# Keys kept in SBUF and chunk values landed by DMA in a hybrid Conformer/RWKV-7 step

## The chip, the core and the metric

The kernel runs on one core of a Trainium2 chip. The metric is device time in microseconds (us) of one execution. The engines are TensorE (PE, with its weight loads as PEld), VectorE (DVE), ScalarE (ACT), GpSimd (POOL) and SyncE (SP). ACT, POOL and SP also issue DMAs; an issue stands in the issuing engine's order of instructions, and in the profile it is listed as ACTq, POOLq or SPq. An engine runs its instructions in order.

## The reference

One inference step of two layers with D = 1024 over 1048 tokens: 16 meta tokens, 1024 prompt tokens and 8 decode tokens. Layer 0 mixes tokens by a Conformer convolution, layer 1 by RWKV-7; each is followed by a squared-ReLU MLP with 4096 hidden features. The change lies in layer 1, whose mixer is, cut to what matters:

```python
xr, xw, xk, xv, xa, xg = (h + (prev - h) * x_mix[i] for i in range(6))
r, k, v = xr @ w_r, xk @ w_k, xv @ w_v
decay = exp(-exp(w_log(xw)));  a = sigmoid(a0 + (xa @ a1) @ a2);  g = sigmoid(xg @ g1) @ g2
kk = k * k_k;  kk = kk / max(norm_per_head(kk), 1e-12)
k = k * (1 + (a - 1) * k_a)
def _wkv7_step(S, inp):                       # per token, per head: S is 64 x 64
    sa = einsum('bhvk,bhk->bhv', S, -kk_t)
    S = S * w_t + sa[..., None] * (kk_t * a_t) + v_t[..., None] * k_t
    y = einsum('bhvk,bhk->bhv', S, r_t)
out = ((groupnorm(y) + sum(r * k * r_k) * v) * g) @ w_o
```

There are 16 heads of 64. All inputs and outputs are float32.

## The kernel before

Layer 0 takes the profile up to about 1128 us. From there to about 1840 us runs the mixer stage of layer 1, the part that the change touches; the MLP of layer 1 follows to the end, and the last chunks of the recurrence run under its first part, up to about 2080 us.

**Groups and blocks.** The mixer stage goes over four token groups (272, 256, 256 and 264 tokens) and in each over 8 blocks `p` of 128 features (`mixer_in`, the loop at L1046). A block computes the projections `pr` (r, copied by ACT at L1049) and `pv` (v, copied to `vv` at L1067), low-rank gate, decay and rate (`l_g`, `l_w`, `l_a` at L964, from `lg`, `lw`, `la`), and from them the operands of the recurrence, which go to DRAM: `d_ab` (four 64-token operands per chunk), `d_v` (values, transposed to token rows: `vt` at L1003, issue L1004; for the meta tokens `vm`, L1007 and L1008), `d_n` (the small matrices to invert), `d_g` and `d_bv`. At block 0 the low-rank projections need `p_wa`, and ACT's `lw` (L954) must be done before PE's `l_w`.

**Keys.** The keys of the next group are computed inside the current one, a block at a time (`keys`, L872): PE projects `pk`, ACT copies it to `st` (L885), issues a DMA to the DRAM tensor `d_k` (L886) and squares it to `sq` (L888); PE sums the squares per head into `pn` (L880), and the group's inverse norms `r16` come from that. In the next group `fetch` loads a block's keys from `d_k` into slot 1 of `rk2` (SP, L1042), one block ahead. DVE then makes `nkk` (L1073, from the keys and the norms), the products `kb` (one multiply of double width, L1092) and `rk` (L1095), and packs `ab` (L1104, L1105).

**Chunks.** The recurrence runs over 17 chunks: chunk 0 holds the meta tokens, the others 64 tokens each. Two operands hold a chunk's values: `sv` is state above values, `uv` is U above values; each has four quarters, a half of 64 partitions for each of two head parities, and the values fill the other half. `front(c)` loads a chunk's operands on SP: `xa`, `bk`, `p` (the inverse) and `vt`, the values as two half tiles (L1185). `chunk(c)` copies them on ACT, two copies into `sv` and two into `uv` (L1246, L1247), then runs W (L1260, reads `sv`), U (into `uv`, L1277 and L1278), S (L1285, reads `uv`), Y (L1292 reads `sv`, L1295 reads `uv`), the output `yt` (L1297) to DRAM `d_y` (two issues, L1300), and the new state into `sv` (L1303, L1306).

**Order.** On PE the mixer stage's matmuls keep the order of the program. `both()` and `fill` inside the projections call `tick`, which moves the inverses (`inverses`, on DVE), the chunks by credits (`RW`, paced by `PACE`) and the output norm on by a step. A chunk can start once its inverse has been issued (`st["inv"]`); after the end of a group the tail of its last block comes in the next group. On the other engines a scheduler orders the instructions; data loads on SP and weight loads share one queue in that order. Buffers come from pools by tag; `bufs` says how many a tag has.

```python
            for p, rk2 in ahead_of(fetch):
                both()
                ps = proj(next(wrkv), act, n, nm("r", p), both)
```

Of the kernel before, what the change touches and what calls it, by code (L numbers as in the profile page):

```python
# [16 lines left out]
P = 128  # L17
D = 1024
KT = D // P
# [29 lines left out]
def hybrid_step(tc, x_prompt, x_sample, state_conv, state_shift, state_wkv, meta_tokens,  # L49
# [10 lines left out]
    with ctx:  # L60
# [15 lines left out]
        d_hn = dram.tile([P, KT, T], F32, name="d_hn")  # L76
        d_k = dram.tile([P, KT, T], F32, name="d_k")
        d_ab = dram.tile([NCH, P, KT, 2, 2 * HS], F32, name="d_ab")
# [714 lines left out]

        prep, norm = {}, {}
        sst = cur["raw"].tile([P, D], F32, name="sst", tag="raw")
# [74 lines left out]
        def keys(g, fill):  # L870

            c0, n = G1[g]  # L872
            nm = lambda s, *a: f"{s}{g}" + "".join(f"_{x}" for x in a)
            mix = prep[g][0]
            act = [mix(2, k) for k in range(KT)]
            pn = bank(nm("pn"), "x")
            add_pn = lambda: None

            def to_pn(p, sq):
                return lambda: nc.tensor.matmul(pn[:, :n], head_sel(p), sq[:, :n], start=p == 0, stop=p == KT - 1)  # L880
            for p in range(KT):
                yield
                ps = proj(next(wrkv), act, n, nm("k", p), fill)
                k_ = pr.tile([P, N1], F32, name=nm("st", p), tag="st", bufs=2)
                nc.scalar.copy(k_[:, :n], ps[:, :n])  # L885
                nc.scalar.dma_start(d_k[:, p, c0:c0 + n], k_[:, :n])  # L886
                sq = pr.tile([P, N1], F32, name=nm("sq", p), tag="rk", bufs=2)
                nc.scalar.activation(sq[:, :n], ps[:, :n], AF.Square, scale=vec("k_k", p))  # L888
                add_pn()
                add_pn = to_pn(p, sq)  # L890
            r16 = lorap.tile([P, N1], F32, name=nm("r16"), tag="lf")
            r16p = norm[g] = [lorap.tile([P, N1], F32R, name=nm("r16" + q), tag="r16" + q, bufs=2)[:, :n] for q in "hl"]
            add_pn()
            nc.vector.tensor_scalar(r16[:, :n], pn[:, :n], L2_EPS * L2_EPS, None, op0=ALU.max)
            nc.scalar.activation(r16[:, :n], r16[:, :n], AF.Sqrt)
            nc.vector.reciprocal(r16[:, :n], r16[:, :n])
            split(*r16p, r16[:, :n], nc.vector)
        carry = {"tail": lambda: None}

        def mixer_in(g, tick):  # L900
# [13 lines left out]
            mix, hx = prep.pop(g)  # L914

            def ahead_of(load):

                nxt = load(0)
                for p in range(KT):
                    cur_, nxt = nxt, load(p + 1) if p + 1 < KT else None  # L920
                    yield p, cur_

# [64 lines left out]
            def finish(p, rk, ab, vv):  # L987
                def trace():
# [45 lines left out]
                    nc.tensor.matmul(pb[:, :n], hsum, rk[:, :n], start=True, stop=True)  # L1034
                    bv = t_("bv", p, "bv", 2)
                    nc.vector.tensor_mul(bv[:, :n], vv[:, :n], pb[:, :n])
                    return lambda: nc.gpsimd.dma_start(d_bv[:, p, c0:c0 + n], bv[:, :n])
                return trace

            def fetch(p):  # L1040
                rk2 = pr.tile([P, 3, N1], F32, name=nm("rk2", p), tag="rk2", bufs=2)
                nc.sync.dma_start(rk2[:, 1, :n], d_k[:, p, c0:c0 + n])  # L1042
                return rk2

            late, later = (lambda: lambda: None), lambda: None
            for p, rk2 in ahead_of(fetch):  # L1046
                both()
                ps = proj(next(wrkv), act, n, nm("r", p), both)
                nc.scalar.copy(rk2[:, 2, :n], ps[:, :n])  # L1049
                if p == 0:  # L1050
                    decay_rate(ww)
                if npr < n:
                    dd(p, 4, rk2[:, 2, npr:n])
                ps = lora2(wg2, p, lg, f"g{p}")
                gt = t_("gt", p, "gt", 2)
                nc.scalar.copy(gt[:, :n], ps[:, :n])
# [12 lines left out]
                later = late()  # L1069
                nkk, kp, rp = (rk2[:, i, :] for i in range(3))  # L1070
                pb = bank(nm("pb", p))
                spread(pb[:, :n], r16p, p)
                nc.vector.scalar_tensor_tensor(nkk[:, :n], kp[:, :n], nvec("k_k", p), pb[:, :n], op0=ALU.mult, op1=ALU.mult)  # L1073
                nc.vector.tensor_tensor_scan(cum[:, :n], smask[:, :n], cum[:, :n], 0.0, op0=ALU.mult, op1=ALU.add)
                em = t_("em", p, "em", 2)
                nc.scalar.activation(em[:, :n], cum[:, :n], AF.Exp, scale=DECAY_SCALE)

                ex = pr.tile([P, 5, HS + 1], F32, name=nm("ex", p), tag="ex", bufs=2)
                nc.gpsimd.memset(ex[:, :, 0:1], 1.0)
# [10 lines left out]

                kb = wa[:, :2, :n]
                nc.vector.tensor_mul(kb, rk2[:, :2, :n], kb)  # L1092
                bb, km = wa[:, 0, :], wa[:, 1, :]
                rk = t_("rk", p, "rk", 2)
                nc.vector.scalar_tensor_tensor(rk[:, :n], rp[:, :n], vec("r_k", p), km[:, :n], op0=ALU.mult, op1=ALU.mult)  # L1095

                ab = pr.tile([P, 5, 4, HS], F32, name=nm("ab", p), tag="ab", bufs=2)
                for s in segs:
                    e = ex[:, s[4]:s[4] + s[2], :s[3]]
                    e = bass.AP(e.tensor, e.offset, [*e.ap[:2], (1, 2), e.ap[2]])  # L1100
                    two = lambda t: t[:, :, s[1]:s[1] + s[2] * s[3]].rearrange("p i (c t) -> p c i t", t=s[3])
                    out = lambda i: ab[:, s[4]:s[4] + s[2], i:i + 2, :s[3]]

                    nc.vector.tensor_mul(out(0), two(rk2[:, 0:3:2, :]), e)  # L1104
                    nc.vector.tensor_mul(out(2), two(wa[:, :2, :]), cols(em, s).unsqueeze(2).broadcast_to([P, s[2], 2, s[3]]))  # L1105
# [64 lines left out]
        def front(c):  # L1170
# [10 lines left out]
            nc.sync.dma_start(p32, d_p[c].rearrange("k r t -> r k t"))  # L1181

            vt = w_([P, KT, HS], "vt", c)
            for q in range(2):
                nc.sync.dma_start(vt[HALF[1 - q]], d_v[c * HS:(c + 1) * HS, :].rearrange("t (k q v) -> q t k v", q=2, v=HS)[q])  # L1185
            yield RW[0]
# [19 lines left out]
            nc.vector.transpose(flat(x32), flat(p32))  # L1206
            chunks[c] = xa, bk, nr, no, p32, x32, vt
            yield RW[2]
# [7 lines left out]
        fronts = {}  # L1216

        def chunk(c):

            while c > st["inv"]:  # L1220
                yield None
            yield from fronts.setdefault(c, front(c))
            xa, bk, nr, no, p32, x32, vt = chunks.pop(c)
            sv, uv = st["sv"], st["uv"]

# [15 lines left out]
            for j in range(2):  # L1241
                nc.vector.tensor_scalar(p64[:, :, 32 * j:32 * j + 32], p32, par32[:, j:j + 1], None, op0=ALU.mult)

            for q in range(2):
                r = HALF[1 - q]
                nc.scalar.copy(sv[r, :, q, :], vt[r])  # L1246
                nc.scalar.copy(uv[r, :, q, :], vt[r])  # L1247

# [37 lines left out]
            if c > 0:  # L1286
# [12 lines left out]
                for q in range(2):  # L1299
                    nc.scalar.dma_start(d_y[t0:t0 + HS].rearrange("t (k q v) -> q t k v", q=2, v=HS)[q], yt[HALF[q]])  # L1300

            fs = w_([P, KT, HS], "fs", c, "w1")
            nc.vector.tensor_mul(fs, kv(ps), wend.broadcast_to([P, KT, HS]))  # L1303
# [341 lines left out]
```

## Time and profile before

| what | value |
|---|---|
| median of 3 runs | 2812.3 us (2811.88 to 2817.02) |
| the profiled execution | 2817.97 us, span 2816.3 us |
| mean granted clock of PE | 0.972 |
| DMA | 416.45 MB, 148 GB/s on average |
| 34 loads `vt` on SP, 68 copies of it on ACT | 0.562 and about 0.617 us each (median) |
| 32 issues `d_k<-st` on ACT | 0.326 us each (median) |
| 32 loads `rk<-d_k` on SP | 0.339 us each (median) |

How to read the rows: a timeline row has start and duration in us, engine, line, operation, out<-in, shape, and in brackets the idle time of that engine just before it, with what ended it. A row of waits has the waiting engine and line, what it waited for, then total us, count and longest. A row of stretches has the window, its length, the busy us of PE, PEld, DVE, ACT and POOL with instruction counts, the granted clock, the share of the DMA engines and GB/s. Lines are those of the kernel before; in the changed kernel the same statements stand up to 14 lines earlier.

### The profile page before, as it was taken

The page shows a single profiled execution, that of the slowest core. Times are in us where ns is not written, and L with a number is a line of the kernel's source. Part 1 is how long each engine was busy: PE and PEld are TensorE (multiplying, and loading weights), DVE is VectorE, ACT ScalarE, POOL GpSimd, SP SyncE. Part 2 cuts the span into 40 slices and gives each one's busy share as a digit, 9 for nine tenths or more (in the row PEclk, how much of TensorE's full clock was granted, in tenths as well). Part 3 has the DMA queues.
Part 4 walks back from the last instruction along what each step waited for, and adds up shares of the span by engine and source line. Part 5 has one row for each costly group of instructions (what it writes and reads, how often), then busy time and mean ns, then how long its engine had stood idle before and what let it go on. Part 6 is the DMA issues. An engine that isn't in the chain of part 4 may idle for free.

```text
span 2816.3 us, 51957 instructions
## 1 busy us (share of the span) xinstructions
PE 2661.4 (95%) x19866; PEld 2510.5 (89%) x19866; DVE 1776.7 (63%) x3518; ACT 1180.9 (42%) x2167; POOL 1499.7 (53%) x2066
## 2 busy tenths in 40 slices
PE   8999999999999899998999999978899999999998
PEld 7998999999999899787787777768789999999998
DVE  5999999996455545233756555488985554444444
ACT  5545444544355333233444453545444452222223
POOL 6676877887788775021111112365568773333332
PEclk9999999999999999999999999979999999999999
DMA  6663544454445642667767766766675642222211
GB/s 178 175 183 90 157 136 135 128 181 135 142 134 157 183 140 83 199 201 203 192 178 199 205 161 181 205 187 177 166 211 154 180 119 86 68 70 73 69 53 42
DMA packets 615863, 416.45 MB, mean 148 GB/s; under 512 B 104936, under 2 KB 558760, under 8 KB 615614
## 3 DMA queue, kind: packets, MB, share of 16 engines
q1 hardware_dynamic: 565996, 367.36, 46.2%
q10 hardware_dynamic: 41090, 19.93, 2.7%
q0 software_dynamic: 8528, 25.83, 2.6%
q8 instruction: 157, 2.57, 0.4%
q14 instruction: 92, 0.75, 0.1%
HBM read 345.60 MB, written 68.37 MB: 147 GB/s over the span
## 4 chain that ended last, share of the span: by engine, by line
PE 72%; DVE 13%; DMA 6%; issue 3%; ACT 3%; POOL 2%; SPq 0%; ACTq 0%; DVEq 0%; POOLq 0%
PE out L187 8%; PE ps_in L189 8%; PE ps_in L187 8%; PE out L189 8%; PE ps_in L188 8%; PE out L188 8%; PE pk L865 3%; PE pr L865 3%; PE pv L865 2%; DVE cv L519 1%; POOL wo_lo L162 1%; PE ps_o L189 1%; DVE tt L1153 1%; PE ps_o L188 1%; PE ps_o L187 1%
## 5 line engine op out<-in xcount | busy, mean ns | idle before, releaser
L162 POOL TENSOR_TENSOR wo_lo<-wo_raw,wo_hi 128x256 fp32r<-128x256 f32 x736 | 564.9, 799 | 259.3 <-ACT wo_hi L157 258.6
L162 POOL TENSOR_TENSOR wi_lo<-wi_raw,wi_hi 128x256 fp32r<-128x256 f32 x640 | 490.1, 798 | 285.5 <-ACT wi_hi L157 267.8
L187 PE MATMUL out<-hh,wo_hi 128*128 128x352 f32 (+2 forms) x1536 | 503.2, 328 | 20.7 <-DVE h L355 9.3
L355 DVE TENSOR_TENSOR h<-h,out 128x352 f32<-128x352 f32 (+2 forms) x768 | 387.3, 510 | 196.8 <-PE out L189 196.4
L189 PE MATMUL out<-hl,wo_hi 128*128 128x352 f32 (+2 forms) x1536 | 494.2, 324 | 7.2 <-DVE hl L141 7.2
L187 PE MATMUL ps_in<-m_h,wi_hi 128*128 128x352 f32 (+2 forms) x1536 | 496.2, 323 | 2.6 <-DVE h L355 2.6
L188 PE MATMUL out<-hh,wo_lo 128*128 128x352 f32 (+2 forms) x1536 | 496.0, 323 | 0.0
L189 PE MATMUL ps_in<-m_l,wi_hi 128*128 128x352 f32 (+2 forms) x1536 | 494.6, 322 | 0.1
L188 PE MATMUL ps_in<-m_h,wi_lo 128*128 128x352 f32 (+2 forms) x1536 | 492.7, 321 | 0.0
L519 DVE SCALAR_TENSOR_TENSOR cv<-u,wdw,cv 128x352 f32<-128x352 f32 (+2 forms) x720 | 376.5, 571 | 0.7
L157 ACT CAST wi_hi<-wi_raw 128x1024 fp32r<-128x1024 f32 x160 | 167.9, 1050 | 398.2 <-PE out L189 198.7
L157 ACT CAST wo_hi<-wo_raw 128x1024 fp32r<-128x1024 f32 x184 | 192.6, 1049 | 316.2 <-PE out L189 154.9
L187 PEld LDWEIGHTS out<-hh,wo_hi 128*128 128x128 f32 x1536 | 293.3, 191 | 26.9 <-DVE h L355 11.7
L189 PEld LDWEIGHTS out<-hl,wo_hi 128*128 128x128 f32 x1536 | 291.2, 190 | 8.9 <-DVE hl L141 8.8
L187 PEld LDWEIGHTS ps_in<-m_h,wi_hi 128*128 128x128 f32 x1536 | 290.0, 189 | 5.2 <-issue 1.7
L188 PEld LDWEIGHTS out<-hh,wo_lo 128*128 128x128 f32 x1536 | 292.8, 191 | 0.6
L188 PEld LDWEIGHTS ps_in<-m_h,wi_lo 128*128 128x128 f32 x1536 | 289.4, 188 | 0.9
L189 PEld LDWEIGHTS ps_in<-m_l,wi_hi 128*128 128x128 f32 x1536 | 288.6, 188 | 1.2 <-DVE m_l L285 0.4
L342 DVE SCALAR_TENSOR_TENSOR r<-ps_in,rs_m 128x352 f32<-128x352 f32 (+2 forms) x192 | 98.2, 515 | 243.3 <-PE ps_in L189 238.1
L141 DVE TENSOR_TENSOR hl<-s,hh 128x352 fp32r<-128x352 f32 (+2 forms) x192 | 147.9, 772 | 104.5 <-ACT hh L140 104.3
L344 ACT ACTIVATE s<-r 128x352 f32<-128x352 f32 (+2 forms) x192 | 93.6, 490 | 128.9 <-DVE r L342 128.5
L1030 POOL DMA_DIRECT2D d_n<-n x32 | 24.4, 764 | 212.9 <-DVE n L1020 141.0
(355 smaller groups left out, 4909.3 us busy)
## 6 DMA issues: line engine op xcount, KB each, us to landing
wi_raw<-in_w_mlp_in_dram SPq DMA_DIRECT2D x160, 512.0 KB
wo_raw<-in_w_mlp_out_dram SPq DMA_DIRECT2D x160, 512.0 KB
wk_raw<-in_rwkv_w_k_dram SPq DMA_DIRECT2D x32, 512.0 KB
wr_raw<-in_rwkv_w_r_dram SPq DMA_DIRECT2D x32, 512.0 KB
wv_raw<-in_rwkv_w_v_dram SPq DMA_DIRECT2D x32, 512.0 KB
d_ab<-ab POOLq DMA_DIRECT2D x32, 512.0 KB, 4.8
pg_raw<-in_conv_w_pw_dram SPq DMA_DIRECT2D x24, 512.0 KB
pa_raw<-in_conv_w_pw_dram SPq DMA_DIRECT2D x24, 512.0 KB
```

What stands on the lines that cost most here:

```text
L141: eng_lo.tensor_sub(lo, src, hi.bitcast(F32))
L157: nc.scalar.copy(hi[:, :a * b], raw[:, :a * b])
L162: eng_lo.tensor_sub(lo[:, cs], raw[:, cs], hi[:, cs].bitcast(F32))
L187: nc.tensor.matmul(ps, w[0], act[0], start=first, stop=False)
L188: nc.tensor.matmul(ps, w[1], act[0], start=False, stop=False)
L189: nc.tensor.matmul(ps, w[0], act[1], start=False, stop=last)
L342: nc.vector.scalar_tensor_tensor(r[:, :n], ps[:, :n], 0.0, rs()[:, :n], op0=ALU.max, op1=ALU.mult)
L344: nc.scalar.activation(s[:, :n], r[:, :n], AF.Square)
L355: nc.vector.tensor_add(hv[:, 4 * i + m, :], hv[:, 4 * i + m, :], ps[:, :n])
L519: nc.vector.scalar_tensor_tensor(acc[m][:, :n], ug[:, m, j:j + n], wdw[:, m, j:j + 1], acc[m][:, :n], op0=ALU.mult, op1=ALU.add)
L865: nc.tensor.matmul(ps[:, :n], w[:, k, :], act[k], start=k == 0, stop=k == KT - 1)
L1153: nc.vector.tensor_mul(o, ni[:, :j, j:j + 1].broadcast_to([B, j, wd]), ni[:, j:j + 1, j + 1:top].broadcast_to([B, j, wd]))
```

## The change

The keys stay in SBUF. `d_k`, its 32 issues on ACT, its 32 loads on SP, `fetch` and `ahead_of` are gone; `st` has nine buffers instead of two, and `rk2` has two slots instead of three. As keys and `nkk` no longer lie side by side, the double multiply `kb` becomes two of 256 columns, `km` and `bb`. Four tags (`gt`, `bv`, `em`, `ex`) go from two buffers to one. The tile `vt` of a chunk, its loads on SP and the copies on ACT are gone; `values(c)` issues four DMAs on ACT instead, from `d_v` straight into the halves of `sv` and `uv`. It is called at a chunk's start, where that had not been done before, and for the next chunk behind Y and the output of the current one.

```diff
-                k_ = pr.tile([P, N1], F32, name=nm("st", p), tag="st", bufs=2)
+                k_ = kept[g, p] = pr.tile([P, N1], F32, name=nm("st", p), tag="st", bufs=KT + 1)
                 nc.scalar.copy(k_[:, :n], ps[:, :n])
-                nc.scalar.dma_start(d_k[:, p, c0:c0 + n], k_[:, :n])
...
-            def fetch(p):
-                rk2 = pr.tile([P, 3, N1], F32, name=nm("rk2", p), tag="rk2", bufs=2)
-                nc.sync.dma_start(rk2[:, 1, :n], d_k[:, p, c0:c0 + n])
-                return rk2
...
-            for p, rk2 in ahead_of(fetch):
+            for p in range(KT):
                 both()
                 ps = proj(next(wrkv), act, n, nm("r", p), both)
-                nc.scalar.copy(rk2[:, 2, :n], ps[:, :n])
+                rk2 = pr.tile([P, 2, N1], F32, name=nm("rk2", p), tag="rk2", bufs=2)
+                nc.scalar.copy(rk2[:, 1, :n], ps[:, :n])
...
-                gt = t_("gt", p, "gt", 2)
+                gt = t_("gt", p)
...
-                nkk, kp, rp = (rk2[:, i, :] for i in range(3))
+                nkk, rp = (rk2[:, i, :] for i in range(2))
+                kp = kept.pop((g, p))
...
-                kb = wa[:, :2, :n]
-                nc.vector.tensor_mul(kb, rk2[:, :2, :n], kb)
                 bb, km = wa[:, 0, :], wa[:, 1, :]
+                nc.vector.tensor_mul(km[:, :n], kp[:, :n], am[:, :n])
+                nc.vector.tensor_mul(bb[:, :n], nkk[:, :n], nav[:, :n])
...
-            vt = w_([P, KT, HS], "vt", c)
-            for q in range(2):
-                nc.sync.dma_start(vt[HALF[1 - q]], d_v[c * HS:(c + 1) * HS, :].rearrange("t (k q v) -> q t k v", q=2, v=HS)[q])
...
+        landed = set()
+
+        def values(c):
+
+            if c < NCH and c <= st["inv"] and c not in landed:
+                landed.add(c)
+                src = d_v[c * HS:(c + 1) * HS, :].rearrange("t (k q v) -> q t k v", q=2, v=HS)
+                for t in (st["sv"], st["uv"]):
+                    for q in range(2):
+                        nc.scalar.dma_start(t[HALF[1 - q], :, q, :], src[q])
+
         def chunk(c):
 
             while c > st["inv"]:
                 yield None
+            sv, uv = st["sv"], st["uv"]
+            values(c)
             yield from fronts.setdefault(c, front(c))
...
-            for q in range(2):
-                r = HALF[1 - q]
-                nc.scalar.copy(sv[r, :, q, :], vt[r])
-                nc.scalar.copy(uv[r, :, q, :], vt[r])
...
+            values(c + 1)
             fs = w_([P, KT, HS], "fs", c, "w1")
```

The order of the matmuls on PE stays the same; on the other engines the scheduler's order moves. Three places show it. First ACT at the first group boundary, about 1318 us in the profile: before, between the last store of group 0's values and `lw` of group 1.

```order
L1004 DMA d_v<-vt_7_13900 128x2x128
L1007 COPY vm_7_13906<-vt_7_13899 16x128
L1008 DMA d_v<-vm_7_13906 16x128
L1049 COPY rk_0_13957<-pr_0_13965 128x256
L1246 COPY sv<-vt_14134 64x8x64
L1247 COPY uv<-vt_14134 64x8x64
L1246 COPY sv<-vt_14134 64x8x64
L1247 COPY uv<-vt_14134 64x8x64
```

And now:

```order
L995 DMA d_v<-vt_7_13883 128x2x128
L998 COPY vm_7_13889<-vt_7_13882 16x128
L999 DMA d_v<-vm_7_13889 16x128
L1211 DMA sv<-d_v 64x8x64 x2
L1036 COPY rk_0_13974<-pr_0_13944 128x256
L1211 DMA uv<-d_v 64x8x64 x2
L945 ACTIVATE lw<-p_wa 64x256
```

Four issues stand where the four copies of chunk 0's values stood; `lw` is the next row behind the copies in the kernel before too (L954). Second, SP at the same place, before (`hx` are the tokens of group 2, `ni` the matrices of the inverse):

```order
L934 DMA wa_3_raw<-d_lr 128x512
L1185 DMA vt_14134<-d_v 64x8x64
L1147 DMA ni_13961<-d_n 32x1024
L146 DMA wr_2_raw<-in_rwkv_w_r_dram 128x8x128
L1185 DMA vt_14134<-d_v 64x8x64
L934 DMA g_0_raw<-d_lr 128x512
L934 DMA g_1_raw<-d_lr 128x512
L1185 DMA vt_14631<-d_v 64x8x64 x2
L934 DMA g_2_raw<-d_lr 128x512
L828 DMA hx_14083<-d_hn 128x8x257
```

And now:

```order
L925 DMA wa_3_raw<-d_lr 128x512
L1135 DMA ni_13940<-d_n 32x1024
L145 DMA wr_2_raw<-in_rwkv_w_r_dram 128x8x128
L925 DMA g_0_raw<-d_lr 128x512
L925 DMA g_1_raw<-d_lr 128x512
L925 DMA g_2_raw<-d_lr 128x512
L827 DMA hx_14064<-d_hn 128x8x257
```

The loads `vt` of chunks 0 and 1 no longer stand ahead of `ni` and `hx`. Third, ACT at the end of chunk 7, before:

```order
L1246 COPY sv<-vt_17490 64x8x64 x2
L1247 COPY uv<-vt_17490 64x8x64 x2
L1297 COPY yt_17705<-Y_17672 128x512
L1197 COPY no_17487<-A_17713 32x128
L1300 DMA d_y<-yt_17705 512x1x64
```

And now:

```order
L1211 DMA sv<-d_v 64x8x64 x2
L1288 COPY yt_17646<-Y_17613 128x512
L1211 DMA uv<-d_v 64x8x64
L1291 DMA d_y<-yt_17646 512x1x64 x2
L1181 COPY no_17429<-A_17658 32x128
```

Two issues stand ahead of `yt` in place of the four copies, and the other two come among the rows behind it. Where the keys are made, `sq` now follows `st` without a row between them.

More of the change, by code (lines that the diff above doesn't have):

```diff
@@ L76, in hybrid_step @@
         d_hn = dram.tile([P, KT, T], F32, name="d_hn")
-        d_k = dram.tile([P, KT, T], F32, name="d_k")
         d_ab = dram.tile([NCH, P, KT, 2, 2 * HS], F32, name="d_ab")
@@ L792, in hybrid_step @@
         wa2 = second([(HALF[0], rwkv_w2[0]), (HALF[1], rwkv_a2[0])], "wa2")
-        prep, norm = {}, {}
+        prep, norm, kept = {}, {}, {}
         sst = cur["raw"].tile([P, D], F32, name="sst", tag="raw")
@@ L914, in mixer_in @@
             mix, hx = prep.pop(g)
[L916 to L921, printed above, removed]
             def mixed(i):
@@ L1034, in trace @@
                     nc.tensor.matmul(pb[:, :n], hsum, rk[:, :n], start=True, stop=True)
-                    bv = t_("bv", p, "bv", 2)
+                    bv = t_("bv", p)
                     nc.vector.tensor_mul(bv[:, :n], vv[:, :n], pb[:, :n])
@@ L1052, in mixer_in @@
                 if npr < n:
-                    dd(p, 4, rk2[:, 2, npr:n])
+                    dd(p, 4, rk2[:, 1, npr:n])
                 ps = lora2(wg2, p, lg, f"g{p}")
-                gt = t_("gt", p, "gt", 2)
+                gt = t_("gt", p)
                 nc.scalar.copy(gt[:, :n], ps[:, :n])
@@ L1074, in mixer_in @@
                 nc.vector.tensor_tensor_scan(cum[:, :n], smask[:, :n], cum[:, :n], 0.0, op0=ALU.mult, op1=ALU.add)
-                em = t_("em", p, "em", 2)
+                em = t_("em", p)
                 nc.scalar.activation(em[:, :n], cum[:, :n], AF.Exp, scale=DECAY_SCALE)
-                ex = pr.tile([P, 5, HS + 1], F32, name=nm("ex", p), tag="ex", bufs=2)
+                ex = pr.tile([P, 5, HS + 1], F32, name=nm("ex", p), tag="ex")
                 nc.gpsimd.memset(ex[:, :, 0:1], 1.0)
@@ L1102, in mixer_in @@
                     out = lambda i: ab[:, s[4]:s[4] + s[2], i:i + 2, :s[3]]
-                    nc.vector.tensor_mul(out(0), two(rk2[:, 0:3:2, :]), e)
+                    nc.vector.tensor_mul(out(0), two(rk2), e)
                     nc.vector.tensor_mul(out(2), two(wa[:, :2, :]), cols(em, s).unsqueeze(2).broadcast_to([P, s[2], 2, s[3]]))
@@ L1206, in front @@
             nc.vector.transpose(flat(x32), flat(p32))
-            chunks[c] = xa, bk, nr, no, p32, x32, vt
+            chunks[c] = xa, bk, nr, no, p32, x32
             yield RW[2]
@@ L1221, in chunk @@
                 yield None
+            sv, uv = st["sv"], st["uv"]
+            values(c)
             yield from fronts.setdefault(c, front(c))
-            xa, bk, nr, no, p32, x32, vt = chunks.pop(c)
-            sv, uv = st["sv"], st["uv"]
+            xa, bk, nr, no, p32, x32 = chunks.pop(c)
             def quads(name, pairs, lhs, rhs):
```

## The prediction

> **What bounds the kernel now.** I read the page first: busy shares and the chain that ended last.
>
> ```profile
> span 2816.3 us, 51957 instructions
> PE 2661.4 (95%) x19866; PEld 2510.5 (89%) x19866; DVE 1776.7 (63%) x3518; ACT 1180.9 (42%) x2167; POOL 1499.7 (53%) x2066
> PE 72%; DVE 13%; DMA 6%; issue 3%; ACT 3%; POOL 2%; SPq 0%; ACTq 0%; DVEq 0%; POOLq 0%
> ```
>
> TensorE (PE) is busy for 95% of the span, so a change that leaves its matmuls alone can only win or lose in the other 5%, and in clock lost after a gap. The code that changes runs from about 1128 to 2080 us. So next comes the table of PE's waits for 1100 to 1860 us (total, count, longest) and the busy time by stretches.
>
> ```profile
> PE l_w L964 <- ACT lw L954: 6.7, 1, 6.7
> PE pn L880 <- ACT sq L888: 5.6, 4, 3.4
> PE nn L1018 <- DVE ab L1105: 4.3, 3, 3.4
> PE A L1192 <- DVE nr L1202: 3.2, 1, 3.2
> PE l_a L964 <- DVE rk L1073: 2.5, 2, 1.6
> ```
> ```profile
> 1320.00:1330.00 10.00, 3.31 (x12) 2.50 (x11) 5.28 (x28) 3.69 (x8) 0.26 (x2) 0.81 0.61 154
> 1330.00:1340.00 10.00, 9.79 (x39) 8.04 (x38) 3.13 (x6) 3.68 (x11) 2.01 (x3) 0.85 0.96 297
> 1702.00:1710.00 8.00, 8.00 (x37) 6.87 (x36) 2.31 (x3) 2.25 (x4) 0.00 (x0) 0.81 0.57 151
> 1880.00:2080.00 200.00, 175.69 (x2070) 163.82 (x2066) 184.40 (x364) 99.14 (x191) 114.86 (x129) 0.93 0.63 164
> ```
>
> The first two waits have the removed instructions behind them, as the timelines below show. The others hang on VectorE (DVE). In the stretches the columns are PE, PEld, DVE, ACT and POOL busy, then the granted clock: it falls to 0.81 around both waits. From 1880 on DVE is busy 184 of 200 us and ScalarE (ACT) half of it.
>
> **The change part by part.** *Values, first group boundary (wait A).* The timeline at 1318 us:
>
> ```profile
> 1317.95 0.25 ACT L1007 COPY vm<-vt 16x128 f32<-16x128 f32 x1 [8.91 <-DMA d_v<-vt]
> 1318.23 0.32 ACTq L1008 DMA_DIRECT2D d_v<-vm  x1
> 1318.60 0.37 ACT L1049 COPY rk<-pr 128x256 f32<-128x256 f32 x1 [0.40 <-ACT vm L1007]
> 1319.64 0.52 SPq L1185 DMA_DIRECT2D vt<-d_v  x1
> 1321.05 0.59 PE L964 MATMUL l_g<-lg,wg 128*128 128x256 f32 x2
> 1321.36 0.58 SPq L1185 DMA_DIRECT2D vt<-d_v  x1
> 1326.87 0.62 ACT L1246 COPY sv<-vt 64x512 f32<-64x512 f32 x1 [3.14 <-DMA vt<-d_v]
> 1327.92 0.37 ACT L954 ACTIVATE lw<-p_wa 64x256 f32<-64x256 f32 x1
> 1328.04 1.20 SPq L1185 DMA_DIRECT2D vt<-d_v  x2
> 1328.34 1.22 PE L964 MATMUL l_w<-lw,wa 128*128 128x256 f32 x2 [6.69 <-ACT lw L954]
> 1330.00 0.55 SPq L828 DMA_DIRECT2D hx<-d_hn  x1
> 1330.21 5.03 PE L865 MATMUL pv<-mx,wv_raw 128*128 128x256 f32 x16
> 1335.31 3.62 PE L865 MATMUL pr<-mx,wr_raw 128*128 128x256 f32 x16
> ```
>
> ACT runs in order, and lw stands behind four copies that wait for the values of chunk 0 to land. PE's l_g ends at 1321.64, and PE then idles 6.69 us. Afterwards ACT has four DMA issues in that place, which need no landing of the values but only of d_v<-vm; the old load vt with that same need began at 1319.64. With the row of such issues and that of the copies they replace,
>
> ```profile
> L1185 SPq DMA_DIRECT2D vt<-d_v x34: 512/562/1532, 1319.6 to 2005.4; - x34
> L1246 ACT COPY sv<-vt x34: 614/618/621, 1322.6 to 2037.9; 64x512 f32<-64x512 f32 x34
> ```
>
> four issues take 4 x 0.56 = 2.25 us and the copy rk 0.37, so lw starts at 1319.64 + 2.62 = 1322.3. PE follows lw's start by 0.42 (1327.92 to 1328.34), so l_w starts at 1322.7 instead of 1328.34: **5.6 us** less, and 1.1 us of the wait left. Bounds: nothing, if an issue is held as long as the copies were; 6.7, if lw is not late at all. The long gap also costs clock: 16 matmuls pv take 5.03 us behind it, 16 alike pr 3.62, so **1.4 us** go with it (0 to 1.4).
>
> *Keys.* The last keys of the fourth group (wait B):
>
> ```profile
> 1697.08 0.38 ACT L885 COPY st<-pk 128x264 f32<-128x264 f32 x1 [1.83 <-PE pk L865]
> 1699.98 0.33 ACTq L886 DMA_DIRECT2D d_k<-st  x1
> 1700.35 0.48 ACT L888 ACTIVATE sq<-pk,pvec 128x264 f32<-128x264 f32 x1 [2.89 <-DMA bk<-d_ab]
> 1700.88 0.71 PE L880 MATMUL pn<-sq,hsel 128*128 128x264 f32 x2 [3.39 <-ACT sq L888]
> 1703.19 1.23 PE L943 MATMUL p_g<-hx,g_raw 128*128 128x264 f32 x2
> 1705.23 0.69 PE L943 MATMUL p_g<-hx,g_raw 128*128 128x264 f32 x2
> ```
>
> The issue of d_k waits for bk's transfer to land, and sq stands behind it, and pn behind sq. Without d_k, sq follows st at once: **2.9 us** (0 to 3.4). The clock of 0.81 over the next 8.0 busy us costs 0.19 x 8.0 = **1.5 us** (a pair of p_g took 1.23 against 0.69 later), and 0.5 us of gap will not bring that on.
> [...]
> In two other groups the issue (0.33) alone stands between st and sq:
>
> ```profile
> 1300.38 0.70 PE L880 MATMUL pn<-sq,hsel 128*128 128x256 f32 x2 [0.91 <-ACT sq L888]
> 1499.91 0.70 PE L880 MATMUL pn<-sq,hsel 128*128 128x256 f32 x2 [0.91 <-ACT sq L888]
> ```
>
> Each shrinks by 0.35 with the start that follows: **0.7 us**. The 32 loads rk on SP go too; no matmul waited for them, so I count nothing, though later loads behind them can only start earlier.
>
> *The rest of the values.* At a chunk's end 4 copies x 0.618 = 2.47 us of ACT become 2.25 us of issues in the same place, behind Y: nothing. But an issue on ACT can be held, as d_k was, with yt, no and the next projection's copies behind it. There are 36 more issues on ACT than before (68 new, 32 gone); I allow half of one hold like 2.9 us, **+1.5 us** (0 to 6, two such holds).
>
> *DVE.* The double multiply becomes two:
>
> ```profile
> 1340.82 0.47 DVE L1073 SCALAR_TENSOR_TENSOR rk<-rk,negs,pb 128x256 f32<-128x256 f32 x1
> 1343.98 0.68 DVE L1092 TENSOR_TENSOR wa<-rk,wa 128x512 f32<-128x512 f32 x1
> ```
>
> Two of the half size at 0.47 are 0.94 against 0.68, +0.26 in each of 32 blocks, hidden wherever PE has other work. It shows only where PE waits for ab or rk: five waits above, 1.3 us at most; nothing at least, since km needs no nkk and can fill DVE's pause behind it. I take **+0.6**. The four buffers that go from two to one cost nothing: their next writer comes one block later, some 16 us.
>
> Sum: 5.6 + 1.4 + 2.9 + 1.5 + 0.7 - 1.5 - 0.6 = 10.0 us. The profiled execution took 2817.97 us (span 2816.3 and 1.7 around it), 5.7 over the median of the three runs, 2812.3. So it would come to 2808.0 there, and from the median to **2802.3**.
>
> **The rivals.** *R1, the gain of A comes back.* PE runs 7 us ahead and meets DVE's inverses, whose input ni and next tokens hx came late too. If these are bound by their own landing and not by SP, the wait of A for nr (3.2) grows by 7, and 2.9 + 1.5 + 0.7 - 2.1 = 3.0 us remain: 2809.3. For it: the wait for nr exists. Against it: on SP hx stood behind vt loads at 1328.04 that waited for the copies, and went at 1330.00; without them it moves with PE.
>
> *R2, slower: ACT is held at the new issues.* Place: the end of each of 16 chunks, between Y and yt. Each issue there takes its turn behind an earlier transfer, and ACT runs in order, so lw, vv or uv come late for PE. The price is 16 x h; it eats the gain (12.1 - 0.6 = 11.5) from h = 0.7 us a chunk, and is slower beyond noise from 1.07. With h = 1.3: 20.8 - 11.5 = +9.3, 2821.6; at the 2.89 of wait B each time +35. For it: wait B is such a hold. Against: of the 32 d_k issues this hold alone shows among PE's long waits, and ACT is half idle from 1880 on.
>
> *R3, slower: sv lands too late.* The tightest place:
>
> ```profile
> 1664.44 1.10 PE L1292 MATMUL Y<-sv,xa 128*64 128x64 f32 x32
> 1676.01 1.15 PE L1260 MATMUL W<-sv,xa 128*64 128x64 f32 x32
> ```
>
> From the end of Y, 1665.54, to W of the next chunk lie 10.5 us; the second issue starts 0.56 us in, so a landing of up to 9.9 us is hidden. Landings seen: 5.5 (vt, 1321.36 to 1326.87), and 8.9 that ACT stood idle ahead of vm for d_v<-vt. At 15 us W waits 5.1 and the clock drops for 1.5 more; four such chunks are 26.4 - 10.0 = +16.4, 2828.7.
> [...]
>
> **How the numbers follow.** A measurement of this kernel can tell about 0.2%, 5.6 us, from no change. Forecast 0.66, R1 0.15, R2 0.12, R3 0.07. The forecast's own range goes from all bounds good (5.6 + 1.1 + 1.4 + 3.4 + 1.5 + 0.7 = 13.7, with the 2.5 of l_a gone 16.2: 2796) to six for holds and the full 1.3 for DVE (12.1 - 7.3 = 4.8: 2807.5). R1 lies at 2809.3, R2 starts at 2817.9 and its nearer part reaches 2822. The range 2796 to 2822 leaves out R3, the far half of R2 and a little below. Faster 0.66, same 0.15 (R1), slower 0.19 (R2, R3).
>
> **What would show it.** In the changed profile: the wait of l_w for lw at 1 us or so; pn's longest wait under 1 us; no clock dip near 1330 and 1702; the SP load hx some 6 us earlier. R1 shows as A's wait for nr of some 10 us; R2 as ACT idle before sv, uv or d_y issues until a DMA, with PE waiting for ACT behind it; R3 as W waiting for DMA sv. I am wrong if PE's waits from 1100 to 1860 us do not fall by about 8 us in all, or if PE's waits between 1860 and 2080 grow by more than 3.

## The result, and the profile after

The changed kernel took 2803.45 us (median of five runs, 2802.06 to 2805.7), the kernel before, on the same chip, 2814.73 (2811.88 to 2818.16): a ratio of 0.9958 [0.9946, 0.9970], 11.3 us faster. A second measurement gave 0.9955 [0.9941, 0.9969]. The forecast was 2802.3 with a sum of 10.0. That the number came out is partly luck: its largest term came out at half its size, and pieces that nobody had forecast made up for it. The two profiled executions lie 14.6 us apart by their spans, more than the medians, so the stretches below add up to somewhat more than the 11.3.

The page after, busy times:

```profile
span 2801.7 us, 51779 instructions
PE 2654.4 (95%) x19866; PEld 2502.9 (89%) x19866; DVE 1772.9 (63%) x3550; ACT 1141.9 (41%) x2101; POOL 1497.7 (53%) x2066
```

Rows of PE's waits after, 1100 to 1860 us (total, count, longest):

```profile
PE pb L755 <- ACT vv L1054: 10.7, 6, 4.0
PE pv L864 <- ACT rk L1036: 4.9, 6, 2.0
PE nn L1009 <- DVE ab L1093: 3.2, 1, 3.2
PE l_w L955 <- ACT lw L945: 3.2, 1, 3.2
PE A L1176 <- DVE nr L1186: 2.2, 1, 2.2
PE pn L879 <- ACT sq L886: 2.2, 4, 0.6
PE l_a L955 <- DVE rk L1061: 2.0, 1, 2.0
```

pn's longest wait fell from 3.4 to 0.6, as forecast. The wait of l_w fell from 6.7 to 3.2, not to 1.1. At the head stand waits for ACT's vv, as they did before:

```profile
PE pb L756 <- ACT vv L1067: 11.1, 5, 4.5
```

The prediction's table of the waits before leaves this row out, so l_w and pn, which it calls the first two, were the second and the third. The waits of pv for ACT's rk are new. All rows of this view together: 64.5 us before and 57.5 after, but 64.6 in a second profile of the changed kernel, so this total can't tell the two kernels apart.

**Where the time went.** PE's order is the same in all kernels here but one (*norm's root earlier*, where the transposes yn of the output norm come at other places), so the program can be cut at fixed matmuls: at the first l_w of a block, and at the first W of a chunk. Six cuts matter:

- S: l_w of blocks 0 to 2 of group 0.
- A: l_w of block 7, group 0, to W of chunk 0 (holds wait A).
- C: W of chunk 4 to l_w of block 3, group 2; D: from there to W of chunk 8.
- B: W of chunk 8 to l_w of block 0, group 3 (holds wait B).
- E: W of chunk 13 to W of chunk 16.

Stretches in time, before: length, then PE, PEld, DVE, ACT and POOL busy with counts, granted clock, DMA share, GB/s, for S, A, C, B, E and what follows:

```profile
1184.56:1212.54 27.98, 24.98 (x138) 20.21 (x139) 14.18 (x34) 10.08 (x31) 6.87 (x12) 0.94 0.63 191
1283.80:1360.76 76.96, 64.16 (x424) 51.65 (x422) 41.71 (x118) 25.91 (x66) 13.66 (x24) 0.93 0.71 194
1508.68:1580.00 71.32, 63.33 (x550) 52.93 (x550) 52.09 (x128) 29.23 (x72) 11.29 (x18) 0.93 0.76 217
1676.01:1726.00 49.99, 46.60 (x445) 39.72 (x444) 18.60 (x42) 15.40 (x34) 6.40 (x13) 0.97 0.67 170
1943.45:2055.87 112.42, 96.43 (x1176) 89.15 (x1175) 106.42 (x220) 54.41 (x105) 61.99 (x66) 0.94 0.66 171
2055.87:2816.30 760.43, 741.50 (x4855) 734.82 (x4854) 375.13 (x681) 260.28 (x426) 377.29 (x489) 0.99 0.34 101
```

The same after:

```profile
1185.15:1209.89 24.74, 23.21 (x137) 19.01 (x138) 14.46 (x36) 10.07 (x31) 6.89 (x12) 1.00 0.67 200
1281.16:1354.69 73.53, 64.74 (x423) 52.56 (x421) 41.99 (x122) 23.87 (x62) 13.61 (x24) 0.93 0.76 191
1500.71:1575.08 74.37, 64.01 (x550) 52.27 (x550) 51.70 (x131) 29.16 (x70) 11.24 (x18) 0.93 0.73 200
1671.39:1716.94 45.55, 44.92 (x445) 38.51 (x444) 18.57 (x43) 13.02 (x30) 6.40 (x13) 1.00 0.73 177
1933.78:2040.09 106.31, 94.31 (x1176) 87.71 (x1175) 101.54 (x214) 46.46 (x92) 57.60 (x64) 0.95 0.75 185
2040.09:2801.70 761.61, 741.60 (x4855) 734.52 (x4854) 379.62 (x687) 260.75 (x427) 379.91 (x492) 0.99 0.34 102
```

B lost 4.4 us and its clock went to 1.00. A lost 3.4, half of what it was to lose. S lost 3.2 and E 6.1, which no term of the sum covers; C grew by 3.0. The rows of the other kernels are read in the same way, in us, from one profile each:

| kernel | S | A | C | D | B | E | first l_w to the end |
|---|---|---|---|---|---|---|---|
| before | 28.0 | 77.0 | 71.3 | 96.0 | 50.0 | 112.4 | 1631.7 |
| after | 24.7 | 73.5 | 74.4 | 96.3 | 45.5 | 106.3 | 1616.5 |
| after, repeated | 24.8 | 73.0 | 74.0 | 96.5 | 46.1 | 107.2 | 1615.4 |
| keys alone | 26.3 | 76.5 | 77.0 | 96.3 | 45.5 | 114.2 | 1625.2 |
| values alone | 26.1 | 75.8 | 74.6 | 98.3 | 51.0 | 105.0 | 1628.7 |
| split alone | 26.9 | 77.5 | 77.0 | 96.3 | 49.9 | 112.1 | 1632.0 |
| buffers alone | 26.5 | 76.8 | 72.2 | 96.3 | 50.0 | 112.6 | 1631.8 |
| d_k issue put back | 26.0 | 75.5 | 75.3 | 96.9 | 51.4 | 106.6 | 1625.4 |
| norm's root earlier | 24.8 | 76.1 | 77.4 | 96.8 | 45.9 | 112.7 | 1631.1 |
| values by POOL | 24.6 | 72.3 | 75.3 | 97.3 | 46.1 | 109.0 | 1620.0 |
| copies put back | 24.7 | 74.7 | 73.0 | 95.8 | 45.5 | 104.5 | 1620.3 |
| no root | 24.9 | 72.1 | 73.4 | 89.8 | 45.8 | 108.0 | 1608.0 |
| values by POOL, then ACT | 24.8 | 73.3 | 73.2 | 96.3 | 46.0 | 107.2 | 1611.9 |
| double multiply kept | 25.3 | 73.5 | 74.5 | 98.0 | 45.5 | 107.8 | 1621.6 |

The two profiles of the changed kernel differ by up to 1.3 us in a stretch, so differences below that are not read. The last column is one execution; the verdicts use the timed runs. Two profiles were taken of an execution far below the median of its kernel: keys alone (6.5 us) and double multiply kept (7.5 us), each the fastest of its runs.

### The profile page after: what moved, and what is told of

Its sections match the earlier page's. It is cut to its first block, busy times and chain, and to the rows that moved or that the text cites. A ratio compares the mean times of both kernels' runs of the same rounds, so it can differ in the third digit from the quotient of the medians.

```text
span 2801.7 us, 51779 instructions
## 1 busy us (share of the span) xinstructions
PE 2654.4 (95%) x19866; PEld 2502.9 (89%) x19866; DVE 1772.9 (63%) x3550; ACT 1141.9 (41%) x2101; POOL 1497.7 (53%) x2066
## 5 line engine op out<-in xcount | busy, mean ns | idle before, releaser
L341 DVE SCALAR_TENSOR_TENSOR r<-ps_in,rs_m 128x352 f32<-128x352 f32 (+2 forms) x192 | 98.3, 515 | 245.9 <-PE ps_in L188 240.7
```

The costliest lines, as they stand in the source:

```text
L341: nc.vector.scalar_tensor_tensor(r[:, :n], ps[:, :n], 0.0, rs()[:, :n], op0=ALU.max, op1=ALU.mult)
```

## The experiments

**The parts, one at a time.** Four kernels, each the kernel before with one piece. *Keys alone:* the change without its part on values (`st` in KT buffers).

> The keys' part alone (keys in SBUF, the multiply split in two, four buffers at one; the values still by loads and copies; eight buffers for the keys instead of nine). Theory 1, the sum of waits: -2.9 (sq behind d_k), -1.5 (clock behind it), -0.7 (two short waits), +0.6 (DVE) = about -4.5 us against the kernel before; wait A (l_w for lw) stays near 6.7 us. Theory 2, DVE's shorter chain counts too (km no longer behind nkk): another -3 us at the start of group 0, so about -7.5. If the scheduler's new order is what counts, anything from -10 to +3.

*Values alone:* the change without its part on keys.

> The values' part alone (keys still through DRAM). Theory 1: -5.6 and -1.4 at wait A, +1.5 for holds on ACT: about -5.5 us against the kernel before, with wait B (pn for sq, 3.4 us) still there. Theory 2 (A gives only what the changed kernel's trace shows, 3.5 + 0.6, and the rest comes back as new waits for ACT): -2 to -4. Parts that add up would make keys and values together -11.

*Split alone:*

```
-                kb = wa[:, :2, :n]
-                nc.vector.tensor_mul(kb, rk2[:, :2, :n], kb)
...
+                nc.vector.tensor_mul(km[:, :n], kp[:, :n], am[:, :n])
+                nc.vector.tensor_mul(bb[:, :n], nkk[:, :n], nav[:, :n])
```

> The kernel before with only the double multiply split, km ahead of bb, everything else as it was. Theory 1 (a cost on DVE): +0.6 us, at most +1.3. Theory 2 (the split frees the chain nkk, bb, ab of the other half and of rk): -2 to -3 us, with the offset at the start of group 0 (1195 to 1212 us) as in the changed kernel, where PE came 3.2 us ahead.

*Buffers alone:* `bv`, `gt`, `em` and `ex` with one buffer, as in `bv = t_("bv", p)`.

> The kernel before with only the four tags gt, bv, em and ex at one buffer. Theory 1: nothing, within 1 us. A rival: the writer of the next block waits for the reader of this one on ACT or DVE, 0.3 us in each of 32 blocks, +10 us; or the scheduler's order moves and the time with it by 2 to 5 us either way.

Measured: keys 0.9985 [0.9975, 0.9994], values 0.9994 [0.9985, 1.0002], split 1.0001 [0.9991, 1.0011], buffers 0.9997 [0.9986, 1.0007]. In us of medians that is -4.2, -1.8, +0.6 and -0.3, where the whole change has -11.3. The keys' part is as large as the sum of waits gave (4.5); the values' part is smaller than both of its forecasts, though its interval still holds a gain of up to 4.2. The keys bring all of B (45.5) by themselves and the values all of E (105.0). But keys and split alone lengthen C by 5.7, and values alone win only 1.2 in A, which is within the spread of two profiles. Together A wins 3.4 and C loses 3.0. The parts do not add.

**The change again, the d_k issue, the norm's root, another queue.** *The changed kernel, unaltered:*

> The changed kernel again, beside the next three on the same chip: -11 us against the kernel before, as on the first measurement (-11.3). If keys alone (-4.2) and values alone (-1.8) simply add, -6.

*The d_k issue put back, with nobody reading what it stores:*

```
+                nc.scalar.dma_start(d_k[:, p, c0:c0 + n], k_[:, :n])
```

> The changed kernel with the 32 issues of d_k put back on ACT behind st; nothing reads d_k. Theory 1 (the issue and what it waits for made wait B and the two short ones): +5.1 us against the changed kernel (2.9 + 1.5 + 0.7), with pn's wait for sq back at 3 us or more near 1694 and the clock dip behind it. Theory 2 (the keys gained by the loads that left SP and by DVE's order, not by the issue): +0 to +1.

*Norm's root earlier, so that its table loads fall elsewhere:* one pause of the output norm's generator taken out, behind `nc.scalar.activation(sq[:n], y[:n], AF.Square)`:

```
-                yield 2
```

> The changed kernel with one line taken out of the output norm, a pause between its square and its root, so that the norm's root and the decays' exponentials no longer alternate on ACT (34 table loads of 1.28 us instead of 38; the kernel before has 36). Theory: the changed kernel lost some 5 us between 1560 and 1580 (as laid over the kernel before) to these loads, with PE waiting for ACT's wa and vv and the clock at 0.88; they come back, so -4 to -6 against the changed kernel and about -16 against the kernel before. Rival (the loss there is DVE's or the DMA's): 0, or slower by the gate's work coming in lumps, +2.

*Values by POOL:* the new issues on the other queue.

```
-                        nc.scalar.dma_start(t[HALF[1 - q], :, q, :], src[q])
+                        nc.gpsimd.dma_start(t[HALF[1 - q], :, q, :], src[q])
```

> The changed kernel with the four DMAs of values issued by POOL instead of ACT. If holds of ACT at these issues cost what the sum allowed (1.5) and what the trace shows at rk and yt (up to 5 us of PE waiting for ACT rk), this is -1.5 to -5 against the changed kernel. Rival: issues cost POOL more (0.75 us each by its other issues) and stand ahead of its sw and of d_ab, d_n stores, so W's sw, the inverses and the next group's loads come later: +3 to +8.

Measured: the change again 0.9955 [0.9941, 0.9969], 2803.41 us; d_k put back 0.9980 [0.9967, 0.9992], 2810.67; root earlier 0.9999 [0.9989, 1.0009], 2816.44; values by POOL 0.9955 [0.9941, 0.9970], 2803.31.

The d_k issue alone costs 7.3 us by the medians (the intervals of the two ratios just overlap), and brings wait B back: B is 5.3 to 5.9 us longer than in the two profiles of the changed kernel, and A 2.0 to 2.5. The timeline of that kernel there:

```profile
1698.67 0.33 ACTq L886 DMA_DIRECT2D d_k<-st  x1
1699.04 0.48 ACT L888 ACTIVATE sq<-pk,pvec 128x264 f32<-128x264 f32 x1 [3.27 <-DMA bk<-d_ab]
1699.58 1.25 PE L880 MATMUL pn<-sq,hsel 128*128 128x264 f32 x2 [3.77 <-ACT sq L888]
1700.62 1.09 PE L936 MATMUL p_g<-hx,g_raw 128*128 128x264 f32 x2
```

The same transfer bk releases the issue, sq follows it and pn idles 3.77 us. No other statement was altered, so the mechanism of B is shown: it was the in-order issue that waited. Moving the root was to win 4 to 6 us and lost 13: C stayed long (77.4) and E came out at 112.7. As PE's order differs in this kernel, it doesn't settle by itself whether the table loads lengthen C. With POOL, E is 1.8 to 2.7 us longer (109.0), the other cuts stay within the spread, and there is no net change; both a gain of 1.5 to 5 and a loss of 3 to 8 had been named.

**What E and C hang on.** *Copies put back:* four copies of the old size on ACT in each chunk, beside the new issues, into a tile that nobody reads (and `st` in KT buffers):

```
+            scr = w_([P, 4, P], "scr", c)
+            for q in range(2):
+                r = HALF[1 - q]
+                for _ in range(2):
+                    nc.scalar.copy(scr[r], m_ar[r].unsqueeze(1).broadcast_to([HS, 4, P]))
```

> The changed kernel with four copies of the old size (64x512) added on ACT where the old copies stood, from a constant into a tile that nothing reads; the values still land by DMA (eight buffers for the keys, to make room). It gives ACT its old work back without the old waits. Theory 1: the stretch from W of chunk 13 to W of chunk 16, 106 to 107 us in the changed kernel and 112 before, won its 6 us because ACT lost those copies: it returns to 111 to 113, and the whole is +6 to +8 against the changed kernel. Theory 2 (the stretch won by another order of DVE's decode work): it stays at 105 to 108, and the whole is +0 to +3. In this kernel the root of the norm doesn't stand between the two decay projections of a block, so W of chunk 4 to l_w of block 3 of group 2, 74 us in the changed kernel and 71.3 before, should read 71 to 72 if that order cost it.

*No root:* `AF.Identity` for `AF.Sqrt` in the output norm.

> The changed kernel with the norm's root replaced by a linear function, which leaves the root out of the output norm: 26 table loads on ACT instead of 38, the order otherwise as the scheduler then makes it. Theory (the alternation of root and exponentials on ACT costs about 5 us between 1500 and 1580): the stretch from W of chunk 4 to l_w of block 3 of group 2 falls from 74 to 69 to 71 us, and the whole by 5 to 10 us against the changed kernel. Rival (PE's waits there are for DVE and the DMA of d_z): the stretch stays at 73 to 75.

*Values by POOL up to chunk 11, then by ACT:*

```
-                        nc.scalar.dma_start(t[HALF[1 - q], :, q, :], src[q])
+                        (nc.gpsimd if c <= 11 else nc.scalar).dma_start(t[HALF[1 - q], :, q, :], src[q])
```

> The changed kernel with the values of chunks 0 to 11 issued by POOL, which is a fifth busy there, and those of chunks 12 to 16 by ACT as before. With POOL throughout the mixer stage was some 3 us shorter and the last chunks 4 to 6 us longer; if these add, -3 to -4 against the changed kernel, about -15 against the kernel before. Wait A (l_w for lw) should be under 1 us. Rival: the stage gain was chance of one profile, 0.

*Double multiply kept:* `rk2` has three slots again, POOL copies the kept keys into one, and the two half multiplies are one again (`st` in KT buffers):

```
+                nc.gpsimd.tensor_copy(rk2[:, 1, :n], kept.pop((g, p))[:, :n])
...
+                kb = wa[:, :2, :n]
+                nc.vector.tensor_mul(kb, rk2[:, :2, :n], kb)
```

> The changed kernel with the double multiply kept: POOL copies a block's keys from their SBUF tile into slot 1 of rk2 (three slots again, eight buffers for the keys), so that DVE multiplies once in double width. Theory 1 (the split brings on the longer stretch from W of chunk 4 to l_w of block 3 of group 2: 71.3 us before, 77.0 with the split alone, 74 in the changed kernel): the stretch reads 71 to 72 and the whole is 2 to 4 us shorter than the changed kernel, unless group 0's first blocks (24.8 us, 28.0 before) go back to 26 to 27, which would make it 0 to 2. Theory 2 (any new order on ACT brings it on): 73 to 75, and the whole within 2 us of the changed kernel.

Measured: copies put back 1.0003 [0.9994, 1.0012], no root 0.9914 [0.9900, 0.9927], POOL then ACT 0.9931 [0.9917, 0.9945], double multiply kept 0.9984 [0.9975, 0.9993].

*Copies put back* doesn't test what it was meant to. The copies depend on nothing, so the scheduler could move them, and all 68 ran ahead of the first chunk:

```profile
L1244 ACT COPY scr<-m_ar x68: 606/616/619, 1125.8 to 1174.4; 64x512 f32<-64x512 f32 x68
```
```profile
1133.69 14.11 ACT L1244 COPY scr<-m_ar 64x512 f32<-64x512 f32 x22
```
```profile
1148.52 1.27 PE L879 MATMUL pn<-sq,hsel 128*128 128x272 f32 x2 [11.29 <-ACT sq L886]
```

The st and sq of the first keys stand behind 22 of them, and pn waits 11.29 us, ahead of everything compared here. In its stretch E there are none (same columns as above):

```profile
1948.00:2052.55 104.55, 93.31 (x1175) 86.97 (x1174) 101.19 (x214) 46.01 (x92) 58.46 (x64) 0.97 0.76 186
```

ACT has 92 instructions and 46 us there, as in the changed kernel, against 105 and 54.4 before. So whether the copies that ACT lost made E shorter is not tested. The table speaks for the values' part: E is 112.1 to 114.2 us in the four kernels that have the copies there (before, keys, split and buffers alone), and 104.5 to 109.0 in the others, except with the norm's root earlier, where ACT has 46.5 us and E is 112.7, in another order of PE. DVE goes along with E as well: it works 106.4 to 107.5 us within the long stretches and 101.2 to 105.5 within the short ones, and is busy for 94 to 97% of each. Of the six instructions fewer on DVE after, three are residual sums that DVE adds behind filler matmuls (29 before, 26 after). Of the 4.9 us of DVE that the changed kernel saves in E, 4.5 turn up behind it (375.13 to 379.62), where PE is busy for 97% and E's gain costs 1.2. Less work on ACT and another order on DVE are both left as the cause of the short E; no run here parts them. C reads 73.0 in this kernel, between the two expectations.

*No root* hits D instead of C: 96.3 to 89.8, and C from 74.4 only to 73.4 where 69 to 71 was expected. With the double multiply kept C stays at 74.5. So taking away the table loads, or the split, doesn't shorten C; the kernels other than before gave 72 to 77, and the cause stays open. With the double multiply kept the kernel is also some 8 us slower than the changed one (0.9984 against 0.9955), which neither expectation had; its profile, of the fastest of its runs, doesn't show where.

*POOL then ACT* is the fastest here that keeps the root, 2796.78 us, 19.5 below the kernel before measured beside it. Against the changed kernel's 0.9955 and 0.9958 it is about 7 us better; its interval overlaps the first of these a little and not the second. The six cuts don't hold the gain; the stretches from W of chunk 0 to W of chunk 4 (142.8 against 146.0 and 144.7) and from l_w of block 0, group 3, to W of chunk 13 (214.0 against 216.8 and 216.1) are 2 to 3 us shorter each. Its timeline at the first group boundary:

```profile
1315.38 0.55 SPq L827 DMA_DIRECT2D hx<-d_hn  x1
1315.77 0.70 PE L955 MATMUL l_w<-lw,wa 128*128 128x256 f32 x2
1328.47 0.43 DVE L831 TENSOR_TENSOR xx<-hx 128x256 f32<-128x256 f32 x1 [7.40 <-DMA hx<-d_hn]
1332.06 0.46 DVE L1061 SCALAR_TENSOR_TENSOR rk<-st,negs,pb 128x256 f32<-128x256 f32 x1
1332.58 1.22 PE L955 MATMUL l_a<-la,wa 128*128 128x256 f32 x2 [7.67 <-DVE rk L1061]
```

l_w no longer waits at all, and yet A is 73.3: PE arrives early, and l_a waits 7.67 us for rk, which stands on DVE behind xx, which waits for the next tokens hx. This is the forecast's rival R1 at work, through hx and not through the wait for nr. In all fourteen profiles W of chunk 0 starts 22.4 to 23.4 us behind the first xx, whether l_w waited or not, so by these rows the landing of hx sets the end of A.

## Why the prediction came out, and where it did not

**Wait B: right, by its steps.** The timeline after:

```profile
1692.69 0.38 ACT L884 COPY st<-pk 128x264 f32<-128x264 f32 x1 [2.06 <-PE pk L864]
1692.97 0.49 ACT L886 ACTIVATE sq<-pk,pvec 128x264 f32<-128x264 f32 x1
1693.51 0.71 PE L879 MATMUL pn<-sq,hsel 128*128 128x264 f32 x2 [0.63 <-ACT sq L886]
1694.06 0.61 PE L934 MATMUL p_g<-hx,g_raw 128*128 128x264 f32 x2
```

sq follows st, pn waits 0.63 and the p_g pair runs in 0.61 where it took 1.23. Forecast 2.9 + 1.5 = 4.4; stretch B lost 4.4 (3.9 in the repeated profile), and 3.9 to 4.5 in every kernel without the d_k issue. The two short waits of pn shrank from 0.91 to 0.56 and 0.57, the forecast's 0.7 in all.

**Wait A: the mechanism of the wait right, its size and what it brings off.** The first failed step is "which need no landing of the values but only of d_v<-vm; the old load vt with that same need began at 1319.64". That start was 1.1 us behind the end of the d_v issue (1318.55), and I took it for the landing's price. The timeline after:

```profile
1316.57 0.32 ACTq L999 DMA_DIRECT2D d_v<-vm  x1
1319.30 0.59 PE L955 MATMUL l_g<-lg,wg 128*128 128x256 f32 x2
1319.96 1.27 ACTq L1211 DMA_DIRECT2D sv<-d_v  x2
1321.27 0.37 ACT L1036 COPY rk<-pr 128x256 f32<-128x256 f32 x1 [4.74 <-issue]
1321.30 1.30 ACTq L1211 DMA_DIRECT2D uv<-d_v  x2
1322.64 0.38 ACT L945 ACTIVATE lw<-p_wa 64x256 f32<-64x256 f32 x1 [1.00 <-issue]
1323.07 1.21 PE L955 MATMUL l_w<-lw,wa 128*128 128x256 f32 x2 [3.18 <-ACT lw L945]
1324.82 0.56 SPq L827 DMA_DIRECT2D hx<-d_hn  x1
1324.93 4.41 PE L864 MATMUL pv<-mx,wv_raw 128*128 128x256 f32 x16
1329.42 3.61 PE L864 MATMUL pr<-mx,wr_raw 128*128 128x256 f32 x16
1335.91 0.70 PE L955 MATMUL l_a<-la,wa 128*128 128x256 f32 x2 [2.01 <-DVE rk L1061]
```

The first new issue goes 1319.96 - 1316.89 = 3.07 us behind the end of the store's issue, not 1.1 (3.16 in the repeated profile), and lw, rk and PE wait behind it. Between the store's issue and its reader the DMA engines moved 6 GB/s before and 266 after, since the loads of wr and g no longer stand behind vt on SP; whether this traffic made the issue go later, no run parts. The wait lost 6.69 - 3.18 = 3.5 us instead of 5.6. The clock of pv came back by 5.03 - 4.41 = 0.6 instead of 1.4 (granted 0.72 before, 0.82 after), behind the gap of 3.18 that remains. And l_a then waits 2.01 for DVE (4.21 in the repeat), where it waited 1.55 before. The pv behind that wait, before:

```profile
1341.88 2.75 PE L865 MATMUL pv<-mx,wv_raw 128*128 128x256 f32 x12
```

And after, so that the clock is lost there instead (granted 1.00 over that row before, 0.62 after):

```profile
1336.45 4.44 PE L864 MATMUL pv<-mx,wv_raw 128*128 128x256 f32 x12
```

The sum 5.6 + 1.4 was forecast; the stretch lost 3.4 (4.0 in the repeat). The second failed step is that the sum lets all of l_w's gain reach the end of the stretch. What reaches it is the gain of hx, before:

```profile
1337.56 2.94 DVE L832 TENSOR_TENSOR xx<-hx 128x256 f32<-128x256 f32 x6 [5.54 <-DMA hx<-d_hn]
```

And after:

```profile
1331.80 0.43 DVE L831 TENSOR_TENSOR xx<-hx 128x256 f32<-128x256 f32 x1 [4.45 <-DMA hx<-d_hn]
```

Counted from the start of A, the first xx starts at 53.8 us before and at 50.6 after; W of chunk 0 follows it by 23.2 and 22.9 us.

**R1** came in part, by another wait than the one it named. The wait for nr fell (3.2 to 2.2) instead of growing to 10, but l_a waits 2.01 after, 4.21 in the repeat, and 7.67 where l_w no longer waits. The prediction argued "on SP hx stood behind vt loads ... without them it moves with PE". It did move with PE, by 5.2 us (1330.00 to 1324.82). But hx is 1 MB, DVE got it 7.6 us behind its issue before, 7.0 after and 13.1 with POOL then ACT (1315.38 to 1328.47), and that landing is what PE next runs into.

**Holds on ACT (+1.5)** are there, but could not be confirmed as a size. ACT's waits after, 1354 to 2040 us, show two that end behind new issues:

```profile
ACT rk L1036 <- issue: 7.1, 1, 7.1
ACT st L884 <- issue: 6.9, 2, 6.6
```

The repeat has both (6.9 and 6.6); the kernel before has none as long at these lines, and with POOL there is none. Each is more than the 2.9 I took as one hold, half counted, but PE had other matmuls at both places and did not stop. The first issue of uv ahead of st goes at 1368.74, when S, which reads uv, has just ended (1368.71), so that hold waited for the tile and not for a transfer. What PE waited for ACT's rk and vv (at pv and pb, 1100 to 1860 us) is 11.1 us before, 15.6 after and 16.3 in the repeat, 5.4 with all values on POOL and 7.1 with POOL up to chunk 11. The last is about 7 us faster than the changed kernel; but with all values on POOL the holds are gone as well and nothing is won. So R2's mechanism is there and did not decide; its price in the kernel's time stays open.

**R3** did not occur: no row of PE's waits after has W behind sv.

**DVE's split (+0.6) and the buffers (0)** were within their bounds: +0.3 [-2.5, +3.1] and -0.8 [-3.9, +2.0], by the ratios.

**What the sum did not have:** S -3.2, E -6.1 (with 1.2 given back), C +3.0, and -1.9 from W of chunk 0 to W of chunk 4. S's gain is partly there in each part alone (1.1 to 1.9) and its clock rises from 0.94 to 1.00; why was not tried. The forecast's 10.0 and the measured 11.3 agree because A's missing 3.6 was more than made up by S and E less C, and the rest of their surplus is the larger distance of the two profiled executions. I had costed every edit on its own rows and nothing for the new order that the edits give to work they do not touch.

The signs I named: pn's longest wait is under 1 us, hx is issued 5.2 us earlier where some 6 was asked, and the clock of 1702 to 1710 us is whole (0.81 before, 1.00 after). The wait of l_w is 3.2 and not 1, and the clock of 1320 to 1330 and 1330 to 1340 us is still 0.83 and 0.84 (0.81 and 0.85 before). PE's waits to 1860 us fell by 7.0 where about 8 was asked, and by nothing in the repeat; those from 1860 to 2080 grew by 1.2 (29.3 to 30.5; 25.5 in the repeat), under the limit of 3. The two windows are fixed in time, and the changed kernel is some 9 us ahead where they meet, so they hold other work than before and were a weak sign.

## What to carry to other kernels

An issue on ACT that waited for a transfer held the work behind it here like a wait of that engine (3.27 us in front of sq and 3.77 in front of PE's pn, d_k put back): look up what stands behind such an issue, and price it where the same engine reads behind the same store and with the traffic that the change will bring there (3.07 us with 266 GB/s; what the traffic and the queue each add, no run parts), not from the start of another engine's load (1.1 us with 6 GB/s). When a long wait goes, list which input the next matmuls need and when it lands (hx here, used 7.0 to 13.1 us behind its issue); the gain was cut there. With a scheduler in between, parts measured alone do not add up: cut the program at fixed points of the bounding engine and compare stretches, and expect stretches that no term of your sum names to move, here by 3 to 6 us. Work that is added as a test has to depend on something, or the scheduler moves it: look up where it ran before you read the result.

## What the runs showed of the hardware

**Clock after short gaps.** A gap of 3.77 us in front of pn (d_k put back) left the p_g pair at 1.09 against 0.61 in the changed kernel, where the gap of 3.18 us in A left pv's 16 matmuls at 4.41 (granted clock 0.82) against 3.61 for pr's 16 behind them (1.00). Behind a gap of 0.63 in the changed kernel the p_g pair took the 0.61, at a clock of 1.00. Nor was pv slower behind a gap of 3.32 in the repeat, at the same place as the 3.18:

```profile
1319.56 0.70 PE L955 MATMUL l_w<-lw,wa 128*128 128x256 f32 x2 [3.32 <-ACT lw L945]
1320.53 3.62 PE L864 MATMUL pv<-mx,wv_raw 128*128 128x256 f32 x16
```

And the gap of 2.01 in front of l_a was followed by 4.44 for pv's 12 matmuls at a clock of 0.62, where the kernel before, behind a gap of 1.55, took 2.75 at 1.00. So the length of a gap alone doesn't tell, in these rows, what clock it costs.

**Table loads.** Rows of ScalarE's groups after, for the two lines that alternate:

```profile
L1436 ACT ACT_TABLE_LOAD x7 | 9.0, 1283 | 0.1
L1050 ACT ACT_TABLE_LOAD x4 | 5.1, 1283 | 0.1
```

Without the root ACT has 26 loads instead of 38, 12 x 1.283 = 15.4 us of ACT, and the kernel is some 10 us faster (2793.21 against 2803.41, measured on two chips), most of it in D.

**Landing.** Behind the end of the issue of the small store d_v<-vm its reader on ACT went 3.07 and 3.16 us later in the two profiles of the changed kernel, the old load on SP 1.1 us later before, with 266 and 6 GB/s moving in the first and the last case.
